# Closing products of a four-layer trunk: weight units of 256 columns over 4 row tiles, or of 512 columns over 2

## The chip, the cores and the metric

The kernel runs on one core of a Trainium2 chip, in one launch. The metric is device microseconds (us) of that core, as the median of repeated runs. The engines are named as in the profile: PE is TensorE's matmul, PEld its weight load, DVE is VectorE, ACT is ScalarE, POOL is GpSimd, SP is the queue that issues all DMAs here.

## What is computed

One inference step of a trunk of four layers over 640 tokens (128 context, 512 latent), 1024 features. Each layer has a token mixer (differential attention, neighbourhood attention, grouped-query attention, Hyena) and then a squared-ReLU MLP, each followed by a gated residual addition and a LayerNorm:

```python
for i in range(DEPTH):                     # 4 layers
    mod = jnp.split(silu(c) @ ada_w[i] + ada_b[i], 6)
    o = mixer_i(modulate(x, mod[0], mod[1]))           # ends in a product with w_o: 1024 x 1024
    x = layer_norm(DN_ALPHA * x + mod[2] * o, ln_g[i, 0], ln_b[i, 0])
    h = modulate(x, mod[3], mod[4])
    f = jnp.square(jax.nn.relu(h @ mlp_w1[i])) @ mlp_w2[i]   # 1024 x 4096, 4096 x 1024
    x = layer_norm(DN_ALPHA * x + mod[5] * f, ln_g[i, 1], ln_b[i, 1])
```

All products with weights are made from high and low parts in float32r, three passes each (`mm3`, L473 to L477): high times high, high times low, low times high.

## The kernel before

**Weight stream.** Every weight matrix is cut on the host into units of 128 x 1024 floats (512 KB). One list, `wlist`, written by `weight_order`, gives the order in which they are used. `wget` takes the next unit and, while at it, has the next `ahead=2` units converted (`w_convert`: ACT copies the high part, L451, DVE or POOL subtracts for the low part, L453) and the ones behind them loaded (`w_issue`, L422, from SP into 3 raw buffers). A converted unit, 128 x 2 x 1024, stands in one of 5 buffers with the tag `hl`. Other things stand there as well: in the MLP of layer 0 the hidden activations of the Hyena filter network (`hab`), which all taps read, and the filter weights being worked on; in the MLPs of layers 1 and 2 the DFT tables.

**Units.** A unit for a feature-major product (`unit_a`: `w1`, `qk`, `hy_in`) has 8 row tiles by 128 columns. A unit for a token-major product (`unit_b`) has 4 row tiles by 256 columns: values, the closing product of the MLP (`w2`), the output projections (`wo`).

**MLP.** The 4096 hidden features go in 8 chunks of 512. For a chunk the four units of `w1` are multiplied (320 tokens per matmul) and their result is squared on ACT and split into `ff`. Then the four units of `w2` of the chunk before are used: for each unit (a quarter q of the 1024 output features) and each of five token tiles t, `w2_group` makes 12 matmuls of 256 columns (4 row tiles, three passes) into one PSUM bank, and `residual` takes it out: DVE multiplies with the gate (L655), then one addition in four on DVE and the others on POOL add to the residual stream (L662). `any1` rotates over four PSUM banks. Between units `side` does the work that the list has there: the adaLN modulation of the next layer (`ada_step`, four DVE instructions of 512 columns for each, L543, ended after 8 by PE, L548), and for the Hyena layer filter weights, taps (`tap_step`, every third group; two matmuls of 512 columns, L1581 and L1582) and DFTs (`hy_dft`).

**Output projections.** They are made in two halves of the features. The first half is a generator (`out_steps`) that gives PE work between attention units: one step, one group (t, q), counted as 1280. The second half and the last chunk of the MLP are made in `sublayer_end`, token tile by token tile, each followed by LayerNorm (`ln_norm`), transposes (L724) and modulation (`ln_out`). For the last token tile `quick` puts all additions on DVE.

**Buffers for short tiles.** 16 buffers of 128 x 640 floats (tag `S`, `self.S`) hold gates, LayerNorm gains, adaLN weights and temporaries. `gtmp`, the product with the gate, has 3 buffers of 256 columns of its own. The framework fixes each engine's order of instructions when the program is built, and an instruction that waits holds up what stands behind it on its engine.

Of the kernel before, what the change touches and what calls it, by code (L numbers as in the profile page):

```python
# [10 lines left out]
F32 = mybir.dt.float32  # L11
# [7 lines left out]
P = 128  # L19
# [10 lines left out]
DEPTH = 4  # L30
# [14 lines left out]
OL0 = 20  # L45
OL1 = 6
# [25 lines left out]
# ---------------------------------------------------------------- host layout and shape constants  # L72
# [127 lines left out]

def prepare(inp):
# [15 lines left out]
    d["w2"] = np.stack([np.stack([unit_b(g["mlp_w2"][l], 4 * ch, q * 256) for ch in range(8) for q in range(4)]) for l in range(DEPTH)])  # L217
# [8 lines left out]
    for nm, wo in (("da", g["da_w_o"][0]), ("na", g["na_w_o"][0]), ("gq", g["gq_w_o"][0][rows]), ("hy", g["hy_w_o"][0])):  # L226
        d[nm + "_o"] = np.stack([unit_b(wo, 4 * kh, q * 256) for kh in range(2) for q in range(4)])
# [51 lines left out]
# ---------------------------------------------------------------- device program  # L279
class Trunk:  # L280
    HL = HLN
    RAW = RAWN
    NS = 16
# [27 lines left out]
    # ---- small helpers  # L311
# [33 lines left out]
    # ---- weight stream  # L345
    def weight_order(self):
        out = []
        for n, l in enumerate(self.layers):
# [46 lines left out]
    def head_order(l):  # L395
        """order of the projections: values of a group of four heads, queries and keys of a pair"""
# [59 lines left out]
    def reach(self, i, n):  # L456
        """end of the first n weights of the stream from i on that need a buffer of it"""
# [14 lines left out]
    # ---- products in three passes  # L472
# [6 lines left out]
    def span_a(self, ps, t, c0, c1):  # L479
        """feature-major product of one unit with tokens c0 to c1; yields now and then"""  # L480
# [6 lines left out]
    # ---- adaLN  # L487
# [30 lines left out]
    def ada_load(self, l, step):  # L518
        """weights of one step: 128 rows (or the bias row) of two neighbouring modulations"""
# [10 lines left out]
    def ada_step(self, raw, l, m, k):  # L530
        """128 rows of a modulation weight times their factors, added up row by row; the sum over partitions ends it"""
# [39 lines left out]
    def ada_gen(self, l, ahead, p0, p1):  # L571
        """pairs p0 to p1 of modulations of a layer; one step per yield, its weights loaded `ahead` steps before"""
# [44 lines left out]
    def load_ln(self, l, j, last=False):  # L617
        """gain and bias of a LayerNorm on all partitions, scaled for the residual stream"""
# [1611 lines left out]
```

## Time and profile before

| | |
|---|---|
| time, median of 3 runs | 3496.15 us (3494.53 to 3499.4) |
| span of the profiled execution | 3487.9 us, 8.25 us under that median |
| busy: PE, PEld, DVE | 3324.3, 3183.9, 2600.0 us |
| busy: ACT, POOL | 1512.3, 1003.6 us |
| matmuls | 25288, as many weight loads |
| mean granted clock of TensorE | 0.986 of full speed |

The span runs from the first to the last instruction of the profiled execution; its own total was not recorded, so what lies around the span is taken as the difference to the median. A matmul's duration in the profile (280 ns for 256 columns) includes its way through the array and overlaps with its neighbours: the rate is read from start to start.

### The profile page before, as it was taken

Reading aid. Unit: us, or ns where it says so; the run is one execution under the profiler, and the core shown is the slowest. Engines: PE = TensorE matmul, PEld = TensorE weight load, DVE = VectorE, ACT = ScalarE, POOL = GpSimd, SP = SyncE. Lnnn points to the kernel's source line nnn. Section 1 sums busy time; section 2 is a strip of 40 time slices with the busy share of each in tenths; the row PEclk is TensorE's granted clock in tenths of the full one; section 3 lists DMA queues with packets and bytes.
Section 4 is the critical chain, followed back from the end, with each engine's and each line's share of the span. In section 5 each row is a group of like instructions: output and inputs, shape, how many; then the busy total and the mean of one; then the engine's idle time right before and its main releaser. Section 6 shows DMA issues by size and latency. Waiting matters only on the chain. (4 is left out here: it accounts for less than half of the span.)

```text
span 3487.9 us, 63715 instructions
## 1 busy us (share of the span) xinstructions
PE 3324.3 (95%) x25288; PEld 3183.9 (91%) x25288; DVE 2600.0 (75%) x4691; ACT 1512.3 (43%) x2700; POOL 1003.6 (29%) x961
## 2 busy tenths in 40 slices
PE   8998999999999989999998999999998999999998
PEld 6878889998999889999988889999998998999998
DVE  4777888788676678777688878777859888945457
ACT  3555453333356654433335665333324333432322
POOL 0333334334354453122252014232334112500002
PEclk9999999999999999999999999999999999999999
DMA  7343134545242324555412112545523224222221
GB/s 271 122 133 108 49 129 165 171 166 175 82 130 77 104 75 158 187 169 197 143 60 69 31 53 94 184 152 182 164 93 123 81 81 152 88 91 79 85 75 54
DMA packets 157644, 418.97 MB, mean 120 GB/s; under 512 B 19550, under 2 KB 29414, under 8 KB 154270
## 3 DMA queue, kind: packets, MB, share of 16 engines
q1 hardware_dynamic: 157344, 414.88, 35.8%
q8 instruction: 199, 3.26, 0.4%
q14 instruction: 101, 0.83, 0.1%
HBM read 371.20 MB, written 34.05 MB: 116 GB/s over the span
## 5 line engine op out<-in xcount | busy, mean ns | idle before, releaser
L662 POOL TENSOR_TENSOR r<-r,gtmp 128x256 f32<-128x256 f32 x444 | 437.8, 999 | 1127.6 <-DVE gtmp L655 1097.3
L453 DVE TENSOR_TENSOR hl<-raw,hl 128x1024 fp32r<-128x1024 f32 x390 | 506.6, 1301 | 322.1 <-ACT hl L451 320.6
L475 PE MATMUL w<-hl,ff 128*128 128x256 f32 x2560 | 716.0, 280 | 7.2 <-DVE gtmp L655 7.1
L476 PE MATMUL w<-hl,ff 128*128 128x256 f32 x2560 | 715.2, 279 | 2.5 <-DVE hl L453 2.4
L477 PE MATMUL w<-hl,ff 128*128 128x256 f32 x2560 | 713.9, 279 | 0.0
L451 ACT CAST hl<-raw 128x1024 fp32r<-128x1024 f32 x411 | 430.2, 1048 | 638.3 <-PE w L477 508.9
L475 PE MATMUL w<-hh,hl 128*128 128x320 f32 (+2 forms) x2048 | 637.7, 312 | 0.2
L476 PE MATMUL w<-hl,hl 128*128 128x320 f32 (+2 forms) x2048 | 634.9, 310 | 1.8 <-DVE hl L736 1.8
L477 PE MATMUL w<-hh,hl 128*128 128x320 f32 (+2 forms) x2048 | 634.3, 310 | 0.0
L475 PEld LDWEIGHTS w<-hl,ff 128*128 128x128 f32 x2560 | 481.0, 188 | 12.1 <-DVE gtmp L655 9.9
L476 PEld LDWEIGHTS w<-hl,ff 128*128 128x128 f32 x2560 | 480.9, 188 | 5.0 <-DVE hl L453 3.3
L477 PEld LDWEIGHTS w<-hl,ff 128*128 128x128 f32 x2560 | 479.9, 187 | 0.0
L543 DVE SCALAR_TENSOR_TENSOR ada<-adaw,sil,ada 128x512 f32<-128x512 f32 x504 | 388.2, 802 | 88.2 <-DMA adaw<-in_ada_w 80.5
L475 PEld LDWEIGHTS w<-hh,hl 128*128 128x128 f32 x2048 | 387.2, 189 | 13.8 <-issue 8.4
L476 PEld LDWEIGHTS w<-hl,hl 128*128 128x128 f32 x2048 | 387.2, 189 | 3.1 <-DVE hl L736 3.0
L477 PEld LDWEIGHTS w<-hh,hl 128*128 128x128 f32 x2048 | 387.0, 189 | 0.8 <-issue 0.8
L655 DVE TENSOR_TENSOR gtmp<-w,gate 128x256 f32<-128x256 f32 x640 | 261.1, 415 | 162.4 <-PE w L477 152.1
L874 ACT ACTIVATE fx<-w 128x640 f32<-128x640 f32 (+2 forms) x136 | 91.6, 673 | 454.2 <-PE w L477 435.3
L475 PE MATMUL qk<-hh,hl 128*128 128x320 f32 (+2 forms) x672 | 216.5, 322 | 6.7 <-DVE gtmp L655 3.9
L476 PE MATMUL qk<-hl,hl 128*128 128x320 f32 (+2 forms) x672 | 211.0, 314 | 0.0
L477 PE MATMUL qk<-hh,hl 128*128 128x320 f32 (+2 forms) x672 | 211.0, 314 | 0.0
L475 PE MATMUL wo<-hl,oh 128*128 128x256 f32 x640 | 184.0, 288 | 8.9 <-DVE gtmp L655 5.8
(344 smaller groups left out, 7132.4 us busy)
## 6 DMA issues: line engine op xcount, KB each, us to landing
raw<-in_w SPq DMA_DIRECT2D x256, 512.0 KB
adaw<-in_ada_w SPq DMA_DIRECT2D x288, 256.0 KB
adaw<-in_ada_w SPq DMA_DIRECT2D x16, 1024.0 KB
raw<-ab_d SPq DMA_DIRECT2D x32, 512.0 KB
raw<-in_hy_in SPq DMA_DIRECT2D x24, 512.0 KB
adaw<-in_ada_s SPq DMA_DIRECT2D x8, 1024.0 KB
raw<-in_da_qk SPq DMA_DIRECT2D x16, 512.0 KB
gate<-gate_d SPq DMA_DIRECT2D x32, 256.0 KB
```

Source lines behind the costliest of these rows:

```text
L451: self.nc.scalar.copy(t[:, 0], raw)
L453: sub(t[:, 1], raw, t[:, 0].bitcast(F32))
L475: mm(ps, w[0], x[0], start=start, stop=False)
L476: mm(ps, w[0], x[1], start=False, stop=False)
L477: mm(ps, w[1], x[0], start=False, stop=stop)
L543: nc.vector.scalar_tensor_tensor(out=y, in0=raw[h], scalar=x, in1=y, op0=ALU.mult, op1=ALU.add)
L655: nc.vector.tensor_mul(tmp, ps, self.gate[2 * s + q // 2][:, (q % 2) * 256:(q % 2) * 256 + 256])
L662: eng.tensor_add(rv, rv, tmp)
L874: nc.scalar.activation(x, src, AF.Relu)
```

## The change

Units of `w2` and of the output projections have 2 row tiles by 512 columns (`unit_w`). A product of a token tile and 512 output columns takes two units, so it is 4 row tiles by three passes again: 12 matmuls, of 512 columns, into one PSUM bank. Gate and residual addition take 512 columns. For the last token tile (`quick`) each half is still made and taken out in two pieces of 256. `gtmp` comes from the `S` buffers, of which there are 17. In the MLP, two units are fetched together and used for five token tiles; the side work comes after the third of the five and at the end, and the list has it after every second unit of `w2`. Steps of the first half of the output projection are twice as large and half as many. The rest of the diff takes comments and docstrings out.

```diff
+def unit_w(w, k0, c0):
+    return w[k0 * P:(k0 + 2) * P, c0:c0 + 512].reshape(2, P, 512).transpose(1, 0, 2).reshape(P, 1024)
...
-    d["w2"] = np.stack([np.stack([unit_b(g["mlp_w2"][l], 4 * ch, q * 256) for ch in range(8) for q in range(4)]) for l in range(DEPTH)])
+    d["w2"] = np.stack([np.stack([unit_w(g["mlp_w2"][l], 4 * ch + 2 * kp, h * 512) for ch in range(8) for h in range(2) for kp in range(2)]) for l in range(DEPTH)])
...
-        d[nm + "_o"] = np.stack([unit_b(wo, 4 * kh, q * 256) for kh in range(2) for q in range(4)])
+        d[nm + "_o"] = np.stack([unit_w(wo, 4 * kh + 2 * kp, h * 512) for kh in range(2) for h in range(2) for kp in range(2)])
...
-    NS = 16
+    NS = 17
...
-                        if 0 < ch < 8:
-                            out += ada[:1] + side[i // 4].get(4 * (ch - 1) + i % 4, [])
-                            ada = ada[1:]
+                        if 0 < ch < 8 and (i < 4 or i % 2):
+                            for n in range(4 * (ch - 1) + (i % 4 if i < 4 else i - 5), 4 * (ch - 1) + i % 4 + 1):
+                                out += ada[:1] + side[i // 4].get(n, [])
+                                ada = ada[1:]
...
+    def wide_group(self, us, x, t, h, quick=False):
+        c = slice(t * P, (t + 1) * P)
+        for c0, w in ((0, 256), (256, 256)) if quick else ((0, 512),):
+            ps = self.any1([P, w], "w2")
+            for k in range(4):
+                u, f = us[k // 2], slice(k % 2 * 512 + c0, k % 2 * 512 + c0 + w)
+                self.mm3(ps, (x[:, 0, k, c], x[:, 1, k, c]), (u[:, 0, f], u[:, 1, f]), k == 0, k == 3)
+            self.residual(ps, t, h, c0, w, quick)
...
-        tmp = self.base.tile([P, 256], F32, tag="gtmp", bufs=3, name=f"gtmp{self.tn}")
-        nc.vector.tensor_mul(tmp, ps, self.gate[2 * s + q // 2][:, (q % 2) * 256:(q % 2) * 256 + 256])
-        rv = self.r[:, t, q * 256:(q + 1) * 256]
+        tmp = self.S(F32, "gtmp", w)
+        nc.vector.tensor_mul(tmp, ps, self.gate[2 * s + h][:, c0:c0 + w])
+        rv = self.r[:, t, h * 512 + c0:h * 512 + c0 + w]
...
-            for q in range(4):
-                u = self.wget(("w2", l, 4 * (ch - 1) + q))
+            for h in range(2):
+                us = [self.wget(("w2", l, 4 * (ch - 1) + 2 * h + kp)) for kp in range(2)]
                 for t in range(NT):
-                    w2_group(u, ch - 1, q, t)
-                    groups += 1
-                    if self.taps and groups % TSTEP == 0:
+                    self.wide_group(us, ff[ch - 1], t, h)
+                    groups += 2
+                    if self.taps and groups % TSTEP < 2:
                         self.tap_step()
+                    if t == 2:
+                        self.side(2)
                 self.side()
...
-    def side(self):
-        while self.wlist[self.wi][0] in ("ada", "hyw", "hyt", "hyd", "hyc"):
+    def side(self, parts=1):
+        n = 0
+        while self.wlist[self.wi + n][0] in ("ada", "hyw", "hyt", "hyd", "hyc"):
+            n += 1
+        for _ in range(-(-n // parts)):
```

In `out_steps` the loop over four quarters becomes a loop over two halves with two units each, and a step counts as 2560; `OL0`, `OL1` and the bounds on `out_left` are halved.

## Rows read from the trace of the kernel before

**Rows 1.** The page, part 1: busy us, share of the span, instructions.
```profile
PE 3324.3 (95%) x25288; PEld 3183.9 (91%) x25288; DVE 2600.0 (75%) x4691; ACT 1512.3 (43%) x2700; POOL 1003.6 (29%) x961
```

**Rows 2.** Windows of three closing stretches: busy us by engine, clock, DMA.
```profile
700.50:733.00 32.50, 31.21 (x254) 30.25 (x252) 30.23 (x53) 11.96 (x17) 17.72 (x17) 1.00 0.48 161
733.00:739.00 6.00, 3.70 (x12) 1.04 (x13) 6.00 (x11) 1.55 (x2) 4.16 (x4) 1.00 0.42 146
1424.00:1456.00 32.00, 30.70 (x257) 30.37 (x256) 30.77 (x48) 8.75 (x10) 15.06 (x13) 1.00 0.49 156
```

**Rows 3.** Groups of PE instructions: busy us, mean ns, idle before and its enders.
```profile
L475 PE MATMUL w<-hl,ff 128*128 128x256 f32 x2560 | 716.0, 280 | 7.2 <-DVE gtmp L655 7.1
L476 PE MATMUL w<-hl,ff 128*128 128x256 f32 x2560 | 715.2, 279 | 2.5 <-DVE hl L453 2.4
...
L475 PE MATMUL wo<-hl,oh 128*128 128x256 f32 x640 | 184.0, 288 | 8.9 <-DVE gtmp L655 5.8 <-ACT oh L1049 2.6 <-ACT o L1128 0.3
...
L548 PE MATMUL ada<-ada,ones 128*32 128x512 f32 x144 | 30.2, 605 | 5.7 <-DVE ada L543 5.6
```

**Rows 4.** Timeline of PE in layer 0: start us, duration us, what.
```profile
704.77 0.40 PE L1581 MATMUL filt<-hl,hab 128*128 128x512 f32 x1
...
705.25 0.28 PE L475 MATMUL w<-hl,ff 128*128 128x256 f32 x1
...
709.49 0.40 PE L1581 MATMUL filt<-hl,hab 128*128 128x512 f32 x1
...
709.95 0.28 PE L475 MATMUL w<-hl,ff 128*128 128x256 f32 x1
...
714.03 0.40 PE L1581 MATMUL filt<-hl,hab 128*128 128x512 f32 x1
...
714.49 0.28 PE L475 MATMUL w<-hl,ff 128*128 128x256 f32 x1
```

**Rows 5.** Timeline of PE in layer 3, where a run of one shape begins.
```profile
3078.26 0.28 PE L475 MATMUL w<-hl,ff 128*128 128x256 f32 x1
...
3106.53 0.31 PE L475 MATMUL w<-hh,hl 128*128 128x320 f32 x1
...
3134.69 0.28 PE L475 MATMUL w<-hl,ff 128*128 128x256 f32 x1
```

**Rows 6.** Groups of DVE instructions by form.
```profile
L543 DVE SCALAR_TENSOR_TENSOR ada<-adaw,sil,ada 128x512 f32<-128x512 f32 x504 | 388.2, 802 | 88.2 <-DMA adaw<-in_ada_w 80.5 <-ACT ln_b L787 6.4 <-ACT ada L541 1.0
L655 DVE TENSOR_TENSOR gtmp<-w,gate 128x256 f32<-128x256 f32 x640 | 261.1, 415 | 162.4 <-PE w L477 152.1 <-POOL r L662 9.9
L662 DVE TENSOR_TENSOR r<-r,gtmp 128x256 f32<-128x256 f32 x336 | 168.5, 503 | 7.7
...
L742 DVE TENSOR_TENSOR r<-r,ln_g 128x512 f32<-128x512 f32 x35 | 29.7, 869 | 0.0
...
L1585 DVE TENSOR_TENSOR win<-win,filt 128x512 f32<-128x512 f32 x40 | 26.9, 673 | 0.3 <-PE filt L1582 0.3
```

**Rows 7.** Groups of POOL instructions by form.
```profile
L662 POOL TENSOR_TENSOR r<-r,gtmp 128x256 f32<-128x256 f32 x444 | 437.8, 999 | 1127.6 <-DVE gtmp L655 1097.3 <-DVE m L2015 24.8 <-DVE rs L693 4.8
...
L753 POOL TENSOR_TENSOR r<-r,ln_g 128x512 f32<-128x512 f32 x8 | 11.1, 1384 | 419.9 <-ACT r L698 419.9
```

**Rows 8.** Waits: us in total, times, longest us.
```profile
ACT hl L451 <- PE w L477: 508.9, 98, 8.4
```

**Rows 9.** Timelines of ACT and of DVE in layer 1: one conversion.
```profile
1432.22 1.05 ACT L451 CAST hl<-raw 128x1024 fp32r<-128x1024 f32 x1 [4.02 <-PE w L477]
...
1434.68 1.75 DVE L453 TENSOR_TENSOR hl<-raw,hl 128x1024 fp32r<-128x1024 f32 x1
```

**Rows 10.** The chain that ended last, end of layer 2's mixer: start us, us.
```profile
2111.88 0.45 PE lnt L724 x4
...
2116.09 1.92 POOL r L662 x2
```

More of the change, by code (lines that the diff above doesn't have):

```diff
@@ L44 @@
 AHD = 1
-OL0 = 20
-OL1 = 6
+OL0 = 10
+OL1 = 3
 WS = (0, 1, 2)
@@ L802, in sublayer_end @@
         self.after = self.spill if spill else self.ln_residual
-    def out_group(self, units, oh, t, qs, quick=False):
-        c = slice(t * P, (t + 1) * P)
-        for q in qs:
-            u = units[q]
-            ps = self.any1([P, 256], "wo")
-            for k in range(4):
-                f = slice(k * 256, (k + 1) * 256)
-                self.mm3(ps, (oh[:, 0, k, c], oh[:, 1, k, c]), (u[:, 0, f], u[:, 1, f]), k == 0, k == 3)
-            self.residual(ps, t, q, quick)
     def out_half(self):
@@ L820, in out_first @@
     def out_first(self, l, nm, split):
-        self.out_left = 4 * NT
+        self.out_left = 2 * NT
         return self.out_steps(l, nm, split)
@@ L833, in out_steps @@
         yield 1
-        for q in range(4):
-            u = {q: self.wget((nm + "_o", q), ahead=1)}
-            if q == 1:
-                self.load_gates(l, 0, (1,))
-                gate.update(self.gate)
-                self.gate = gate
-            for t in range(NT):
-                if q == 0 and t + 2 < NT:
+        for h in range(2):
+            us = [self.wget((nm + "_o", 2 * h + kp), ahead=1) for kp in range(2)]
+            for t in range(NT):
+                if h == 0 and t == 2:
+                    self.load_gates(l, 0, (1,))
+                    gate.update(self.gate)
+                    self.gate = gate
+                if h == 0 and t + 2 < NT:
                     split(oh, 0, t + 2)
-                self.out_group(u, oh, t, (q,))
+                self.wide_group(us, oh, t, h)
                 self.out_left -= 1
-                yield 1280
+                yield 2560
         self.scale_r = False
@@ L850, in out_rest @@
         self.load_ln(l, 0)
-        while self.out_left > 6:
+        while self.out_left > 3:
             next(first)
@@ L860, in out_rest @@
         units = [self.wget((nm + "_o", 4 + q), ahead=1) for q in range(4)]
-        self.sublayer_end(l, 0, lambda t, i: self.out_group(units, oh, t, (2 * i, 2 * i + 1), t == NT - 1))
+        self.sublayer_end(l, 0, lambda t, i: self.wide_group(units[2 * i:2 * i + 2], oh, t, i, t == NT - 1))
     def mlp(self, l, nxt, last):
@@ L907, in w1_first @@
             self.settle()
-        def w2_group(u, ch, q, t, quick=False):
-            ps = self.any1([P, 256], "w2")
-            c = slice(t * P, (t + 1) * P)
-            for kk in range(4):
-                f = slice(kk * 256, (kk + 1) * 256)
-                self.mm3(ps, (ff[ch][:, 0, kk, c], ff[ch][:, 1, kk, c]), (u[:, 0, f], u[:, 1, f]), kk == 0, kk == 3)
-            self.residual(ps, t, q, quick)
         for ch in range(8):
@@ L938, in mlp @@
         units = [self.wget(("w2", l, 28 + q), ahead=1) for q in range(4)]
-        def close(t, i):
-            for q in (2 * i, 2 * i + 1):
-                w2_group(units[q], 7, q, t, t == NT - 1)
-        self.sublayer_end(l, 1, close, last, nxt in (1, 3))
+        self.sublayer_end(l, 1, lambda t, i: self.wide_group(units[2 * i:2 * i + 2], ff[7], t, i, t == NT - 1), last, nxt in (1, 3))
     def v_gen(self, nm, gr, vv, chunks, state):
@@ L1990, in close @@
         self.debt += CRATE
-        while self.debt > 0 and self.k.out_left > 6:
+        while self.debt > 0 and self.k.out_left > 3:
             self.debt -= next(self.first)
```

5 lines of the change are left out of this document (2 added, 3 removed).

## The prediction, made before the changed kernel ran

> **What bounds the kernel now.** I read the page first: PE is busy for 95% of the span and PEld for 91%, DVE for 75% [rows 1]. A busy PE need not be a PE at its rate, so I then took the timeline of PE and looked at starts. In layer 3, 240 matmuls of 256 columns take 28.27 us, 117.8 ns each, and the 192 of 320 columns behind them 28.16 us, 146.7 ns each [rows 5]: back to back, nothing in between. There PE's streaming is the bound. The windows show the second limit: in the closing stretches of layers 0 and 1, DVE is busy for 30.2 of 32.5 us and 30.8 of 32 us, almost as long as PE, and just behind the first of these PE was busy for only 3.7 of 6 us while DVE was busy for all 6 [rows 2]. The groups of PE say what that is worth: the idle time that ends with DVE's gate product or with its adaLN sum is 7.1, 5.8 and 5.6 us [rows 3], 18.5 us in the whole kernel. So little is to be had behind PE; what counts is the rate of PE and what newly holds it up.
>
> **Term 1: matmuls, -7 us.** There are 640 + 160 groups of 12 matmuls [rows 3]. The quick tiles keep 4 groups in each of 8 sublayer ends, 384 matmuls; the other 9216 of 256 columns become 4608 of 512. As many columns are streamed. Only a cost per matmul can be saved, and the rows give it twice. Directly: in layer 0 three pairs of 512-column matmuls of the filter work stand in the stream, 480, 460 and 460 ns a pair [rows 4], 240, 230 and 230 ns each, mean 233.3. The 36 matmuls of 256 columns between them took 117.8 and 113.3 ns each [rows 4]. By a line: from 256 to 320 columns the interval grows by 28.9 ns, 0.452 ns a column, which leaves 2.2 ns fixed and gives 233.4 ns at 512. Two matmuls of 256 cost 235.6 ns, or about 234.8 with layer 0's faster stretches counted in. I take 1.5 ns saved per wide matmul: 4608 x 1.5 = 7 us. Bounds from the same rows: 230 ns would give 4608 x 5.6 = 26 us faster, 240 ns 4608 x 4.4 = 20 us slower.
>
> 4608 weight loads go too. I cost them at nothing: a load runs under the matmul before it, and four transposes of 128 columns start 113 ns apart [rows 10], which is below 117.8. If that cover is thinner than it looks, the gain is the first rival's.
>
> **Term 2: DVE and POOL, -9 us.** 768 gate products of 415 ns [rows 6] become 384 of 512 columns. Their nearest row is a 512-column product out of PSUM, 673 ns [rows 6]: 319 us become 258, 60 saved. The additions on DVE, 503 ns at 256 and some 869 at 512 [rows 6], save perhaps 20 us more. POOL's, 999 ns at 256 and 1384 ns in a 512-column row [rows 7], go from 438 us to some 310. Nearly all of it lies under PE. In one chunk of layer 0 (some 33 us), 20 x 415 ns become 10 x 673, 1.6 us less on an engine that is 93% busy. I give half of the 18.5 us that PE waits for DVE today: 9. Bounds: 0 and 18.5.
>
> **Term 3: sublayer ends, -3 us.** Here the chain runs through DVE and POOL; at the end of layer 2's mixer two POOL additions take 1.92 us of it [rows 10]. One of 512 columns is 1.4 to 1.5 us by rows 7. Seven ends with POOL on the path, 0.4 us each: 3 us. The last token tile is still taken in 256s, so the last wait before the LayerNorm is the same, and so is the kernel's tail. Bounds: 0 and 7.
>
> **Term 4: the weight buffers, +8 us.** This is the cost. A group now needs two units at once, and both are held for five tiles, 14.1 us, where one was held for 7.1. With 5 `hl` buffers, of which layer 0 keeps 2 (activations, filter weights) and layer 1 up to 2 (DFT tables), the pair leaves one to convert ahead. Already ACT's conversions wait 98 times, 508.9 us, for PE to release a buffer [rows 8]; today that is free, since the unit is needed 7 us later. A conversion seen whole took from 1432.22 to 1436.43 us, 4.2 us, because DVE had other work in front [rows 9]. Now the first buffer of a pair is released when PE is half through its last group, 1.4 us before the next half begins. Where nothing was converted ahead the wait is up to 4.2 - 1.4 = 2.8 us. What queues behind it: PE's next products, and on ACT the squares and on DVE the gate products behind the conversion. There are 28 halves in layers 0 and 1, so the bounds are 0 and 78 us. I expect most to have one unit ready; and with four PSUM banks PE can make the first unit's products of the next tiles meanwhile. I take 8 waits of 1 us.
>
> **Term 5: +1 us.** `gtmp` now competes for the `S` buffers that adaLN weights are loaded into; there is one buffer more and about one more in use. DVE already waits 80.5 us for those loads [rows 6]. If they came a tenth later, 8 us would be the price on DVE, under PE in most places. I take 1. **At nothing:** the larger steps between attention units, the adaLN steps that come two to a half (same count), the loads (same bytes through SP, in the same order of use). What hides them is PE's own work: the idle time before `wo` products is 8.9 us in all [rows 3]; coarser steps could double or halve it, 9 us either way.
>
> Sum: -7 - 9 - 3 + 8 + 1 = -10 us. On the span, 3487.9 - 10 = 3478; with the 8.25 us to the median, 3486.
>
> **Rivals.**
>
> *The loads set the pace (3452 us).* If the 117.8 ns are mostly a load (113 ns apart in the transposes, [rows 10]) and not streaming, the wide matmul gains more. The granted clock is at its upper level, 2.4 GHz, in these stretches [rows 2]: 0.417 ns a column; 320 columns then have 13.3 ns of fixed cost, 512 columns take 226.7, and 4608 x 8.9 = 41 us are saved in place of 7: -44 us. For it: PEld's 91%. Against it: no 512-column row is below 230 ns. The Trainium skill (Perfetto Trace Analysis, Identifying the Most-Contended Engine) counts LDWEIGHTS busy time, not matmul busy time, as the measure of how near TensorE is to its limit, and so speaks for this rival; the 512-column rows of this trace speak against it.
>
> *No buffer ahead (3522 us, the other side).* In layers 0 and 1, the pair leaves no converted unit at 20 of the 28 halves, and PE stands for 2.2 us at each: +44 in place of +8, a sum of +26 us. It turns the sign where the waits come to more than 18 us, 0.64 us a half. For it: the 98 waits, and conversions that take 4.2 us. Against it: in layers 2 and 3 there is room, and the order of PE can be bent around a late unit. The Trainium skill (Perfetto Trace Analysis, Optimization Strategy) reads a gap that repeats on the busiest engine as a sign of too few buffers; no such gap stands in the trace of before, it would be new.
>
> *Slow wide stream (3513 us).* All wide matmuls run like the slowest pair, 240 ns: +20 in place of -7, a sum of +17. For it: that pair stands in the 117.8 ns regime, which layer 3 has throughout. Against it: two pairs of three.
>
> *Nothing to measure (3489 to 3503 us).* Streaming the same, DVE's relief off the path or eaten by term 4.
>
> **How the numbers follow.** The forecast, small and faster, has 0.33, with a range of its own of 3468 to 3489; loads 0.10; nothing 0.25; no buffer 0.20; slow stream 0.12. 0.2% is 7 us, about what a measurement of this kernel can tell from no change. Faster: 0.33 + 0.10 = 0.43; same 0.25; slower 0.20 + 0.12 = 0.32. The range, 3458 to 3524, takes in the forecast, no change, and both slower rivals; it leaves out the loads' case and the upper end of term 4, together under 0.2.
>
> **What would show it.** Term 1: starts of `w` matmuls of 512 columns in layer 3 at 233 ns (227 or 240 for the rivals). Term 2: 416 gate products, the 512s near 675 ns, and less idle PE before L548. Term 3: shorter gaps before L724. Term 4: PE idle that ends with DVE's conversion (L453), 2.4 us now in that group of products [rows 3], should rise to some 8; at 40 the buffer rival is right, and the waits would stand in layers 0 and 1 and not in layer 3. The prediction is wrong if the wide interval is off by 3 ns (14 us), or if another order of the engines moves the attention stages by more than the 9 us that I allow.

## The result, and the profile after

The changed kernel takes 3585.87 us (median of 4 runs, 3580.0 to 3589.75) against 3496.8 us (4 runs, 3494.53 to 3499.4): a ratio of 1.026, 95% interval 1.0248 to 1.0272. It is 89 us slower, outside the predicted range of 3458 to 3524. The profiled execution has a span of 3584.6 us, 96.7 more than the one before.

The page, part 1, of the changed kernel:

```profile
PE 3363.5 (94%) x20680; PEld 2987.4 (83%) x20680; DVE 2563.1 (72%) x4145; ACT 1511.0 (42%) x2700; POOL 924.5 (26%) x739
```

Beside [rows 1]: 4608 matmuls and as many loads fewer, as forecast; DVE 37 us and POOL 79 us less busy, where the forecast was some 80 and 128. Yet PE is busy for 39 us *more*, and idle for 57 us more. To see where, take one window from the first `w1` matmul to the last `w2` matmul of each layer. First the kernel before, layers 0 to 3 (window, length, busy us of PE, PEld, DVE, ACT, POOL, clock, DMA):

```profile
440.44:955.09 514.65, 497.33 (x3634) 475.78 (x3633) 406.85 (x652) 206.10 (x298) 188.95 (x176) 0.99 0.45 149
1291.09:1796.24 505.15, 497.26 (x3794) 488.49 (x3793) 383.43 (x569) 198.76 (x275) 147.88 (x135) 0.99 0.47 157
2126.40:2626.79 500.39, 490.35 (x3747) 480.85 (x3745) 376.49 (x564) 190.57 (x262) 153.86 (x135) 1.00 0.45 149
3011.49:3473.24 461.75, 456.41 (x3475) 455.14 (x3472) 266.10 (x460) 140.91 (x189) 36.62 (x24) 0.99 0.23 76
```

The same windows of the changed kernel, and three short ones inside layer 0:

```profile
447.60:1011.86 564.26, 515.56 (x2698) 439.80 (x2697) 405.17 (x555) 207.23 (x297) 172.91 (x118) 0.95 0.41 136
1349.75:1875.78 526.03, 506.17 (x2858) 446.13 (x2857) 382.97 (x472) 198.89 (x275) 124.75 (x77) 0.99 0.46 151
2204.99:2721.35 516.36, 501.65 (x2811) 442.63 (x2809) 380.02 (x467) 190.79 (x262) 123.48 (x77) 0.98 0.43 144
3113.57:3570.87 457.30, 451.72 (x2538) 412.13 (x2537) 243.97 (x307) 141.71 (x191) 40.82 (x26) 0.99 0.24 76
...
489.60:517.60 28.00, 28.00 (x190) 27.78 (x190) 15.70 (x21) 11.43 (x17) 0.00 (x0) 1.00 0.57 194
587.60:643.60 56.00, 51.15 (x233) 39.55 (x232) 42.87 (x59) 18.60 (x25) 20.67 (x15) 0.94 0.47 156
545.60:559.60 14.00, 5.98 (x13) 1.29 (x12) 9.59 (x15) 1.06 (x2) 4.79 (x4) 0.63 0.37 131
```

The MLPs of layers 0, 1 and 2 are 49.6, 20.9 and 16.0 us longer; layer 3's, the only one with no side work (adaLN of a next layer, filter taps, DFTs), is 4.5 us shorter. What lies between the windows, the mixers, grew by 7.2, 1.9, -0.9 and 7.5 us. So the loss is in the MLPs with side work, not in wide products as such.

PE's stream itself did well. From the timeline of PE, where a half of wide products begins and where the next `w1` unit begins, in layer 3 (start us, duration us):

```profile
3182.31 0.40 PE L480 MATMUL w<-hl,ff 128*128 128x512 f32 x1
...
3209.80 0.31 PE L480 MATMUL w<-hh,hl 128*128 128x320 f32 x1
```

120 matmuls in 27.49 us are 229.1 ns each, against 235.6 ns for two of 256 columns [rows 5]: 6.5 ns saved. Layer 3 is the best case. In the MLPs of layers 0 to 2, where nothing held them up, matmuls of 256 columns started 116.6 to 117.4 ns apart and those of 512 229.1 to 229.9, so 3 to 6 ns are saved there, and some 23 us in the whole kernel; 6.5 ns everywhere would be 30. What PE waited for, in groups that answer to [rows 3] (busy us, mean ns, idle before and its enders):

```profile
L481 PE MATMUL w<-hl,ff 128*128 128x512 f32 (+1 forms) x1312 | 510.9, 390 | 7.6 <-DVE hl L458 7.4
L480 PE MATMUL w<-hl,ff 128*128 128x512 f32 (+1 forms) x1312 | 509.7, 389 | 16.7 <-DVE gtmp L669 16.7
...
L553 PE MATMUL ada<-ada,ones 128*32 128x512 f32 x144 | 55.7, 671 | 23.1 <-DVE ada L548 21.2 <-DVE gtmp L669 1.7
```

Waits of PE in the kernel before (us in total, times, longest):

```profile
PE lnt L724 <- ACT r L698: 23.6, 11, 4.5
...
PE w L476 <- DVE hl L736: 1.8, 5, 0.8
```

And PE's waits in the changed kernel:

```profile
PE w L480 <- DVE gtmp L669: 17.1, 13, 4.3
PE w L481 <- DVE hl L750: 13.1, 4, 3.3
...
PE w L480 <- DVE win L1581: 9.7, 4, 4.0
PE lnt L738 <- ACT r L712: 9.2, 4, 2.3
```

At the sublayer ends the wait before the transposes became shorter (23.6 to 9.2 us), but that of the `w1` products behind them for the modulated input became longer (1.8 to 13.1). The adaLN sums (5.6 to 21.2 us) and the gate products (7.1 to 16.7 us, 17.1 with those before `w1` products) got worse. One such stall, in layer 0, on three engines of the changed kernel. The timeline of PE (start us, us, what, idle before and who ended it):

```profile
766.74 0.39 PE L1578 MATMUL filt<-hl,hab 128*128 128x512 f32 x1
771.38 0.80 PE L480 MATMUL w<-hl,ff 128*128 128x512 f32 x1 [4.25 <-DVE gtmp L669]
771.98 0.63 PE L481 MATMUL w<-hl,ff 128*128 128x512 f32 x1
772.40 0.63 PE L482 MATMUL w<-hl,ff 128*128 128x512 f32 x1
```

The timeline of DVE at that place:

```profile
765.05 0.67 DVE L1581 TENSOR_TENSOR win<-win,filt 128x512 f32<-128x512 f32 x1
768.45 0.75 DVE L548 SCALAR_TENSOR_TENSOR ada<-adaw,sil,ada 128x512 f32<-128x512 f32 x1 [2.72 <-DMA adaw<-in_ada_w]
...
770.66 1.27 DVE L669 TENSOR_TENSOR gtmp<-w,gate 128x512 f32<-128x512 f32 x2
```

The timeline of SP's queue ahead of it:

```profile
758.70 0.33 SPq L427 DMA_DIRECT2D raw<-in_w  x1
...
763.34 0.33 SPq L1592 DMA_DIRECT2D abc_d<-ab  x1
763.76 0.38 SPq L427 DMA_DIRECT2D raw<-in_w  x1
764.20 1.40 SPq L437 DMA_DIRECT2D adaw<-in_ada_w  x3
```

And what SP waited for from 758 to 772 us (us in total, times, longest):

```profile
SPq L1592 <- DVE ab L1586: 12.7, 3, 5.1
SPq L427 <- DVE hl L458: 2.9, 1, 2.9
```

Read backwards: PE stands for 4.25 us before a wide product, until the first of two gate products has emptied its bank. DVE has these gate products *behind* adaLN steps: it waits 2.72 us for the weights of one of their instructions, and then does that one, another and parts of a filter tap before the first gate product. SP issued three of those loads only from 764.20 on, behind a store of filter taps and a raw weight load. The store had waited 3.2 us for DVE before 763.34 (the rest of the 12.7 us falls behind the loads), and the raw load before it, at 758.70, 2.9 us for a conversion by DVE: the ring is closed.

It is not that loads came later on the whole. DVE's wait for adaLN weights in the changed kernel (us in total, times, longest), against 80.5 us before [rows 6]:

```profile
DVE ada L548 <- DMA adaw<-in_ada_w: 73.3, 31, 7.4
```

What grew is PE's wait behind DVE.

The clock adds to it. From 762.0 to 766.7 us the granted clock was 1.00; from 771.3 to 775.0, behind the stall, it was 0.56, and PE's matmuls start 0.42 us apart (771.98 to 772.40), not 0.23. Around 546 us, where PE was busy for 6.0 of 14 us, it was 0.63; over layer 0's MLP it was 0.95, before 0.99. With two levels, 2.4 and 1.2 GHz, the clock records of the two traces give 51 us of this stage at the lower one, in place of 10. PE is busy there for 18.2 us more and idle for 31.4 us more. So about a third of this stage's 49.6 us, or a little more, is slower matmuls, and the rest is standing (an estimate from these windows).

### The profile page after: what moved, and what is told of

Read it like the earlier page. It is cut to its first block, busy times and chain, and to the rows that moved or that the text cites. A ratio compares the mean times of both kernels' runs of the same rounds, so it can differ in the third digit from the quotient of the medians.

```text
span 3584.6 us, 53289 instructions
## 1 busy us (share of the span) xinstructions
PE 3363.5 (94%) x20680; PEld 2987.4 (83%) x20680; DVE 2563.1 (72%) x4145; ACT 1511.0 (42%) x2700; POOL 924.5 (26%) x739
## 4 chain that ended last, share of the span: by engine, by line
PE 54%; DVE 16%; issue 4%; POOL 3%; ACT 2%; DMA 2%; SPq 0%; DVEq 0%; POOLq 0%; ACTq 0%
PE w L481 12%; PE w L480 12%; PE w L482 12%; DVE ada L548 2%; DVE gtmp L669 2%; DVE hl L458 2%; PE s L2006 2%; PE pv L2053 2%; PE ptp L1057 2%; POOL r L676 2%; PE qk L480 1%; PE qk L481 1%; PE qk L482 1%; DVE r L676 1%; DVE hl L750 1%
## 5 line engine op out<-in xcount | busy, mean ns | idle before, releaser
L676 POOL TENSOR_TENSOR r<-r,gtmp 128x512 f32<-128x512 f32 x222 | 353.3, 1596 | 1286.4 <-DVE gtmp L669 1249.5
L480 PE MATMUL w<-hh,hl 128*128 128x320 f32 (+2 forms) x2048 | 645.1, 315 | 11.0 <-DVE win L1581 9.7
L481 PE MATMUL w<-hl,hl 128*128 128x320 f32 (+2 forms) x2048 | 642.6, 314 | 13.1 <-DVE hl L750 13.1
L482 PE MATMUL w<-hh,hl 128*128 128x320 f32 (+2 forms) x2048 | 641.6, 313 | 1.9 <-DVE hl L458 1.9
L480 PE MATMUL w<-hl,ff 128*128 128x512 f32 (+1 forms) x1312 | 509.7, 389 | 16.7 <-DVE gtmp L669 16.7
L481 PE MATMUL w<-hl,ff 128*128 128x512 f32 (+1 forms) x1312 | 510.9, 390 | 7.6 <-DVE hl L458 7.4
L482 PE MATMUL w<-hl,ff 128*128 128x512 f32 (+1 forms) x1312 | 509.5, 389 | 0.0
L548 DVE SCALAR_TENSOR_TENSOR ada<-adaw,sil,ada 128x512 f32<-128x512 f32 x504 | 414.2, 864 | 80.6 <-DMA adaw<-in_ada_w 73.3
L480 PEld LDWEIGHTS w<-hh,hl 128*128 128x128 f32 x2048 | 392.5, 192 | 29.3 <-DVE win L1581 13.2
L482 PEld LDWEIGHTS w<-hh,hl 128*128 128x128 f32 x2048 | 391.9, 191 | 7.5 <-issue 5.0
L669 DVE TENSOR_TENSOR gtmp<-w,gate 128x512 f32<-128x512 f32 (+1 forms) x416 | 272.8, 661 | 103.0 <-PE w L482 102.7
L480 PEld LDWEIGHTS w<-hl,ff 128*128 128x128 f32 x1312 | 247.5, 189 | 77.8 <-DVE gtmp L669 20.8
L481 PEld LDWEIGHTS w<-hl,ff 128*128 128x128 f32 x1312 | 247.8, 189 | 65.1 <-DVE hl L458 13.6
L482 PEld LDWEIGHTS w<-hl,ff 128*128 128x128 f32 x1312 | 247.7, 189 | 53.5 <-issue 4.2
L480 PEld LDWEIGHTS qk<-hh,hl 128*128 128x128 f32 x672 | 129.3, 192 | 23.9 <-issue 19.6
```

Source lines behind the costliest of these rows:

```text
L480: mm(ps, w[0], x[0], start=start, stop=False)
L481: mm(ps, w[0], x[1], start=False, stop=False)
L482: mm(ps, w[1], x[0], start=False, stop=stop)
L548: nc.vector.scalar_tensor_tensor(out=y, in0=raw[h], scalar=x, in1=y, op0=ALU.mult, op1=ALU.add)
L669: nc.vector.tensor_mul(tmp, ps, self.gate[2 * s + h][:, c0:c0 + w])
L676: eng.tensor_add(rv, rv, tmp)
```

## The experiments

In the source of the experiments `W2` and `WO` name the layers whose closing MLP product and output projection are wide, `GT` is the number of buffers that `gtmp` has of its own (0: it comes from `S`), `NS` and `HLN` are the numbers of `S` and of weight buffers. The changed kernel is `W2 = WO = (0, 1, 2, 3)`, `GT = 0`, `NS = 17`, `HLN = 5`; with `W2 = WO = ()`, `GT = 3`, `NS = 16` it is the kernel before. Each diff is against the kernel named. The third column is the difference to runs of the kernel before on the same chip; changes from one kernel to another are taken from this column, where the changed kernel stands at +89.1.

| run | median us | against before | ratio, 95% interval |
|---|---|---|---|
| e1 only `w2` wide | 3576.61 | +81.1 | 1.0236 (1.0222 to 1.0250) |
| e2 only `wo` wide | 3523.70 | +28.2 | 1.0082 (1.0068 to 1.0096) |
| e3 only `w2` of layer 3 wide | 3497.91 | +2.4 | 1.0012 (1.0003 to 1.0021) |
| e4 changed, 256-column matmuls | 3594.21 | +98.7 | 1.0288 (1.0273 to 1.0304) |
| e5 before, `gtmp` in `S` | 3505.66 | +9.6 | 1.0029 (1.0019 to 1.0038) |
| e6 changed, gate in 256s, own buffers | 3577.16 | +81.1 | 1.0229 (1.0212 to 1.0246) |
| e7 before, 4 weight buffers | 3585.60 | +89.5 | 1.0255 (1.0240 to 1.0270) |
| e8 changed, adaLN loads first | 3564.55 | +68.5 | 1.0197 (1.0182 to 1.0212) |
| e9 changed, 14 `S` | 3588.78 | +94.1 | 1.0275 (1.0259 to 1.0290) |
| e10 changed, 14 `S`, 6 weight buffers | 3598.87 | +104.2 | 1.0305 (1.0291 to 1.0318) |
| e11 before, adaLN loads first | 3498.29 | +3.6 | 1.0012 (1.0004 to 1.0021) |
| e12 as e3, gate as before | 3490.86 | -3.8 | 0.9991 (0.9982 to 0.9999) |
| e13 changed, thin adaLN | 3494.09 | -1.0 | 1.0000 (0.9991 to 1.0010) |
| e14 before, thin adaLN | 3463.79 | -31.3 | 0.9908 (0.9893 to 0.9923) |
| e15 before, pair list | 3562.32 | +67.2 | 1.0186 (1.0171 to 1.0202) |
| e16 e6 and e8 together | 3563.20 | +68.1 | 1.0194 (1.0177 to 1.0211) |
| e17 changed, adaLN beside `w1` | 3508.82 | +14.8 | 1.0043 (1.0029 to 1.0058) |
| e18 as e12, adaLN beside `w1` | 3469.12 | -24.9 | 0.9929 (0.9916 to 0.9941) |

### Which part of the change (e1 to e4)

```diff
 e1, against the changed kernel
-WO = (0, 1, 2, 3)
+WO = ()
 e2, against the changed kernel
-W2 = (0, 1, 2, 3)
+W2 = ()
```

> The changed kernel with the output projections as before (units of 256 columns, steps of 1280); the closing MLP product stays wide. By stage, the changed kernel lost 82 us in the MLPs and 14 us in the mixers and ends. If all the loss of the MLPs comes from the wide MLP product itself (theories A, buffers, and B, side work, alike), this kernel stands near 3572 us, 14 less than the changed one. If the wide projections also spoil the MLPs that follow, by a shifted order of the engines, it stands below 3555.

> The kernel before with only the output projections wide. Both theories leave the MLPs alone here: 3496 + 14 = 3510 us if the mixers' loss stays, 3490 if the loss of the mixers was only a late start that the MLPs handed on (1152 wide matmuls at some 6.5 ns saved each are 7 us).

The wide MLP product alone costs 81 us, the wide projections alone 28; they don't add up to 89, so the parts share a cost. e2 came out above both of its forecasts: its MLPs, narrow as before, did not stay as they were, layer 0's was 14 us longer and layer 1's 10. (The 1152 wide matmuls in its forecast should be 864.)

```diff
 e3, against the changed kernel
-W2 = (0, 1, 2, 3)
-WO = (0, 1, 2, 3)
+W2 = (3,)
+WO = ()
```

> The kernel before with only the closing MLP product of layer 3 wide. That MLP has no side work, and no buffer is kept for activations or tables. A (a pair of units leaves too few weight buffers, everywhere) would show some of the loss here too: 3496 to 3510 us. B (the loss is that of side work standing beside the pairs) gives the streaming gain alone, 864 wide matmuls x 6.5 ns = 5.6 us: 3491 us. In the changed kernel this stage was 4.4 us shorter.

Layer 0's and layer 3's MLP in this kernel:

```profile
443.57:970.75 527.18, 498.68 (x3634) 482.43 (x3633) 401.58 (x652) 206.70 (x298) 193.71 (x176) 0.97 0.43 146
...
3027.43:3483.01 455.58, 450.22 (x2539) 410.68 (x2536) 242.73 (x308) 141.29 (x190) 37.88 (x24) 0.99 0.23 77
```

By its time alone e3 would speak for theory A. The windows say otherwise: layer 3 gains 6.2 us, all that the stream should bring (its MLP has 936 wide matmuls, not 864: 936 x 6.5 = 6.1). But layer 0, narrow in every instruction, loses 12.5: something other than width and pairs came with the change.

```diff
 e4, against the changed kernel, in wide_group
-            for k in range(4):
-                u, f = us[k // 2], slice(k % 2 * 512 + c0, k % 2 * 512 + c0 + w)
-                self.mm3(ps, ...
+            for d in range(0, w, 256):
+                for k in range(4):
+                    u, f = us[k // 2], slice(k % 2 * 512 + c0 + d, k % 2 * 512 + c0 + d + 256)
+                    self.mm3(ps[:, d:d + 256], ...
```

> The changed kernel in everything (pairs of units, 512-column bank, 512-column gate product and addition, side work in the same places, S buffers), but each wide matmul is made as two of 256 columns. If the loss comes with the staging (A and B), the 30 us that the wide stream saved go as well: 3586 + 30 = 3616 us. If the wide matmuls are themselves what costs (fewer, longer instructions, more of the clock's lower level), this kernel comes back towards before: under 3520 us.

Only 10 us slower than the changed kernel, between the two forecasts. So wide matmuls are not the trouble, and of what they save, 23 to 30 us, the larger part had been lost already. Layer 3's MLP gives back 5 us here; layer 0's is even 8 us shorter than in the changed kernel.

### Theory A: too few weight buffers (e7, e9, e10)

```diff
 e7, against the kernel before
-HLN = 5
+HLN = 4
 e9, against the changed kernel
-NS = 17
+NS = 14
 e10, against e9
-HLN = 5
+HLN = 6
```

> The kernel before with 4 weight buffers in place of 5 and nothing else. Holding two units of the closing product in place of one takes one buffer away during that product. A: taking one away for good costs the narrow kernel as much or more: 3550 us or above, with layer 0's MLP (which keeps activations in one) hit first. If the number of buffers is not what hurts: 3496 to 3510 us.

> The changed kernel with 14 S buffers in place of 17 and nothing else: the control for the next kernel, which needs the room. C (short tiles are scarce, and scarcer with the gate product among them): slower than the changed kernel, 3590 to 3620 us. If S buffers are not scarce: 3580 to 3590.

> The changed kernel with 6 weight buffers and 14 S buffers: against the control it has one weight buffer more and no other difference. A (the pair holds one buffer too many; one buffer is worth 90 us to the narrow kernel): 40 to 80 us less than the control. B (late side work alone): within 15 us of the control.

e7 looked like a proof: one buffer fewer costs the narrow kernel 89.5 us. But its loss stands elsewhere: 21 us in layer 0's MLP, 30 in layer 1's, none in layer 2's, and 10, 17, 5 and 12 in the mixers. e9 is 5 us slower than the changed kernel, so three `S` buffers are worth little there. And e10 takes the proof back: one weight buffer *more* does not help the wide kernel, it is 10 us slower than its control. The wait in question (us in total, times, longest), in e9:

```profile
ACT hl L462 <- PE w L488: 482.3, 119, 14.1
```

And in e10:

```profile
ACT hl L462 <- PE w L488: 442.0, 107, 14.7
```

The conversions wait 40 us less for PE, and nothing comes of it; the kernel before has 508.9 us of this wait [rows 8] and is the faster one. Theory A falls as the cause of this loss; whether a sixth buffer helps once the adaLN steps are moved (e17) was not run. The Trainium skill (Perfetto Trace Analysis, Optimization Strategy) says that a gap repeating on the busiest engine can mean too few buffers; here a gap stands in six chunks of layer 0 (PE busy for 6.0 to 11.7 of 14 us in the worst window of each), and the buffer nearest at hand was not the cause.

### Theory C: the short tiles (e5, e6, e12)

```diff
 e5, against the kernel before
-NS, GT = 16, 3
+NS, GT = 17, 0
 e6, against the changed kernel (its wide_group); e12, against e3
-NS, GT = 17, 0
+NS, GT = 16, 3
...
-            self.residual(ps, t, h, c0, w, quick)
+            for d in range(0, w, 256):
+                self.residual(ps[:, d:d + 256], t, h, c0 + d, 256, quick)
```

> The kernel before with one edit: the 256-column product with the gate comes from the S buffers, of which there are 17, in place of 3 buffers of its own. Where only layer 3's MLP was made wide, and where only the projections were, the MLP of layer 0 was 12.5 and 14.2 us longer although it was narrow; what it shared with the changed kernel was this. C (the shared short-tile buffers cost by themselves): 3496 plus 12 to 22 us, 3508 to 3518, with layer 0's MLP some 12 us longer. If those 12 us were an accident of a shifted order of the engines: 3496 us, within 5.

Layer 0's MLP in e5:

```profile
443.14:971.29 528.15, 499.60 (x3634) 483.75 (x3633) 401.08 (x652) 206.77 (x297) 194.48 (x176) 0.97 0.43 146
```

It is 13.5 us longer than before, and the kernel 9.6 us (lower than expected, since layer 2's MLP came out 5.5 us shorter). The cost that term 5 of the prediction names is real.

> The changed kernel with wide matmuls and pairs of units, but the product with the gate and the addition in two pieces of 256 columns, in 3 buffers of their own, with 16 S buffers as before. C: the sharing's cost goes, 12 to 22 us less than the changed kernel, 3564 to 3574 us. A (pairs leave too few weight buffers) and B (side work) keep the rest of the 90 us. If the wide eviction relieved DVE by what term 2 said, 9 us come back on top: 3573 to 3583. If the sharing and the wide eviction together were the whole loss, under 3510.

8 us better than the changed kernel, a little short of the mark, and the mixers come back. The windows of layers 0, 2 and 3 in e6:

```profile
443.93:996.84 552.91, 507.09 (x2698) 435.61 (x2697) 409.83 (x653) 208.18 (x298) 190.18 (x177) 0.97 0.41 139
...
2195.30:2714.55 519.25, 499.81 (x2810) 440.89 (x2809) 387.81 (x565) 190.54 (x262) 135.66 (x136) 0.98 0.42 144
3099.39:3558.00 458.61, 450.93 (x2538) 411.26 (x2537) 250.68 (x457) 140.90 (x190) 38.23 (x24) 0.99 0.22 76
```

Layer 0's mixer ends 3.5 us after the time of before, not 7.2, and layer 3's takes 384.84 us, as before (384.70), not 392.22. e6 changes two things at once, the buffers and the width of the pieces; e5, with the buffers alone, made these two mixers 2.7 and 5.8 us longer, so most of it is the buffers. The MLPs stay slow.

> The kernel before with the closing MLP product of layer 3 alone in wide matmuls and pairs; the gate product and the addition stay in pieces of 256 columns with their own 3 buffers, and 16 S buffers stay. The wide MLP of layer 3 was 6.2 us shorter, and the shared S buffers cost 10 us by themselves. A and C together: 3496 - 6 = 3490 us, faster than both kernels. If the shared buffers were not what cost in the layer 3 experiment: 3497.

3.8 us faster than the kernel before, with an interval that just leaves out 1; the forecast of 3490 held.

### Theory B: side work that comes late (e8, e11, e16, e15)

```diff
 e8, against the changed kernel; e11, against the kernel before; e16, against e6 (in wget)
+        self.ada_issue(self.reach(self.wi, AAH) )
         self.w_convert(self.reach(i + 1, ahead))
         self.w_issue(self.reach(self.w_cv, raws))
-        self.ada_issue(self.reach(self.wi, AAH) )
```

> The changed kernel with one edit: the loads of the adaLN weights are issued ahead of the conversions and raw loads of the same step, so that they don't stand behind raw loads that wait for a buffer on SP's queue. B (PE waits in its fixed order for side work that comes late): the 21 us that PE waits for adaLN sums fall to some 6, and with what queues behind them the time to 3560 to 3572 us. A: no change, 3580 to 3590 us.

> The kernel before with the loads of the adaLN weights issued ahead of the conversions and raw loads of the same step. In the changed kernel this edit took 21 us off. If late adaLN loads are a thing that pairs bring (raw loads wait longer for a buffer and hold up SP's queue), the narrow kernel gains at most the 5.6 us that PE waits for adaLN sums: 3490 to 3497 us. If the order on SP was simply bad in both: 3475 to 3485.

21 us come back in the changed kernel, and PE's waits for adaLN sums fall to 13.9 us:

```profile
PE ada L559 <- DVE ada L554: 13.9, 9, 4.5
```

DVE's own wait for these loads did not fall with it:

```profile
DVE ada L554 <- DMA adaw<-in_ada_w: 83.8, 35, 8.7
```

The same edit does nothing good to the narrow kernel (+3.6 us), in which DVE waits 80.5 us for such loads without it [rows 6]. So late loads are common to both forms, and their sum does not follow the time; in the changed staging PE hangs on them.

> The changed kernel with both edits that helped: gate product and addition in pieces of 256 columns with buffers of their own (9 us less by itself), and adaLN loads issued first (21 us less by itself). If they are separate costs: 3556 us. If they are the same cost seen twice (the S buffers hold up the adaLN loads): 3564 us or more. If the remaining loss hung on both together: under 3530.

With e6's edit on top nothing more is gained (+68.1 in place of +68.5): the two are not separate costs. 68 us remain.

```diff
 e15, against the kernel before
 in weight_order: the list as in the changed kernel (side work behind every second unit of w2)
 in mlp:
             for q in range(4):
-                u = self.wget(("w2", l, 4 * (ch - 1) + q))
+                if q % 2 == 0:
+                    us = [self.wget(("w2", l, 4 * (ch - 1) + q + kp)) for kp in range(2)]
                 for t in range(NT):
-                    self.narrow_group(u, ff[ch - 1], t, q)
+                    self.narrow_group(us[q % 2], ff[ch - 1], t, q)
...
-                self.side()
+                self.side(2 - q % 2)
```

> The kernel before (units of 256 columns, one used after the other, its own gate buffers) with only the fetching of the changed kernel in the MLPs: two units are fetched together, the list has the side work behind every second unit, and it is done after the fifth and the tenth group. A second unit is converted earlier, but the first is free again after five groups as before. If list order and fetching in pairs are the main cost: 3530 to 3560 us. If holding both units for the whole half is what costs, or the width: 3496 to 3510.

The four MLPs of e15:

```profile
447.23:991.06 543.83, 507.96 (x3635) 478.51 (x3633) 406.33 (x652) 207.33 (x298) 186.79 (x176) 0.98 0.43 141
1326.81:1852.53 525.72, 510.07 (x3795) 491.75 (x3793) 384.09 (x569) 198.59 (x276) 142.83 (x135) 0.98 0.46 151
2182.88:2699.99 517.11, 501.18 (x3746) 484.08 (x3745) 380.89 (x564) 190.50 (x263) 146.94 (x135) 0.99 0.43 145
3085.06:3545.84 460.78, 455.32 (x3474) 453.95 (x3473) 266.07 (x459) 140.87 (x189) 36.66 (x24) 0.99 0.24 76
```

Same matmuls, same gate products, same buffers, the same side work in other places: and 67 us lost. Layers 1 and 2 lose 20.6 and 16.7 us, as in the changed kernel (20.9 and 16.0); layer 0 loses 29 of its 50; layer 3, with no side work, nothing. PE's waits for gate products and adaLN sums in e15:

```profile
PE w L486 <- DVE gtmp L688: 22.4, 24, 2.9
PE ada L559 <- DVE ada L554: 16.0, 12, 3.8
```

Together 38.4 us, as in the changed kernel (17.1 and 21.2), where the kernel before has 7.1 and 5.6 [rows 3]. The list and the fetching in pairs are the main cost, and only where there is side work. The two were not run apart from each other.

### The link: adaLN steps on DVE (e13, e14, e17, e18)

```diff
 e13, against the changed kernel; e14, against the kernel before
 in ada_issue:
-            if key[0] == "ada":
+            if key[0] == "ada" and key[3] in (0, KD - 1):
 in ada_step:
-        for h in range(2):
+        for h in range(2) if k in (0, KD - 1) else ():
```

> The changed kernel with six of the eight accumulation steps of each adaLN modulation of layers 1 to 3 left out, with their loads (the first and the last step and the closing sums stay, so the modulations are not those of the reference). B' (DVE, in its fixed order, stands at adaLN steps whose loads come late, and the gate products behind them hold up PE): most of the loss goes, within 30 us of the same omission in the kernel before. If adaLN is not the link, the distance stays at 70 to 90 us.

> The kernel before with the same six of eight adaLN steps and their loads left out (the modulations of layers 1 to 3 are not those of the reference): the other side of the comparison. PE waits 5.6 us for adaLN sums today, and DVE stands before gate products for 12.9 us: 3475 to 3492 us.

With thin adaLN work the distance between the two forms falls from 89 to 30 us: the omission saves the narrow kernel 31 us, more than forecast, and the wide one 90. So some 59 us of the distance hang on adaLN work, and 30 do not.

```diff
 e17, against the changed kernel; e18, against e12 (in weight_order, w2 in pairs, n the place of a unit)
-                                out += ada[:1] + side[i // 4].get(n, [])
-                                ada = ada[1:]
+                                m = 2 - i % 2 if i < 4 else int(n % 4 == 0)
+                                out += ada[:m] + side[i // 4].get(n, [])
+                                ada = ada[m:]
 and likewise where w2 is taken unit by unit
```

> The changed kernel with the adaLN steps moved, none left out: six of them stand behind the four w1 units of a chunk (two and one in turn) and one in the w2 part, in place of four and four. In the changed kernel's layer 0, DVE is busy for 15.7 of 28 us beside w1 (489.6 to 517.6 us of its span) and for 42.9 of 56 us in the two parts that follow a chunk further on; a step is four instructions of 0.86 us, 3.4 us. B' (in the w2 part, with its list in pairs, DVE's steps come late and hold up gate products and with them PE): 3520 to 3550 us. If only the amount of adaLN work on DVE counts, not where it stands: 3575 us or more.

Nothing is left out here, and the changed kernel comes down by 74 us, more than forecast. PE's waits for adaLN sums and gate products in e17:

```profile
PE ada L561 <- DVE ada L556: 7.4, 7, 2.5
...
PE w L488 <- DVE gtmp L690: 3.0, 4, 1.0
```

The windows of the MLPs of layers 0 to 2 in e17:

```profile
447.82:970.10 522.28, 497.03 (x2698) 436.92 (x2697) 402.29 (x555) 206.52 (x297) 165.04 (x118) 0.98 0.44 147
1309.16:1815.65 506.49, 497.54 (x2859) 445.09 (x2857) 371.49 (x472) 198.79 (x275) 117.41 (x77) 0.99 0.47 157
2143.68:2644.63 500.95, 491.42 (x2811) 439.74 (x2809) 365.02 (x467) 190.33 (x262) 117.89 (x77) 0.99 0.44 149
```

21.2 and 17.1 us of waiting became 7.4 and 3.0, and the three MLPs lose 42, 20 and 15 us of length. DVE does the same 504 adaLN instructions; it does fewer of them beside the gate products, and more beside `w1`, where in the changed kernel it was busy for only 15.7 of 28 us. In one chunk of layer 1 they take 8.4 us beside `w1` (1464.89 to 1494.19 us) and 16.4 beside `w2` (1494.19 to 1527.22) in the changed kernel; in e17 13.7 (1475.19 to 1507.57) and 5.4 (1507.57 to 1537.94).

> The kernel of the wide MLP product in layer 3 alone with the gate in pieces of 256 columns (3490.9 us), with the same move of the adaLN steps to the w1 units in layers 0 to 2. Leaving out six of eight steps took 31 us off the kernel before; moving three of eight steps of a chunk to where DVE has room may give a third of that: 3480 us, faster than both kernels. If the steps beside w1 come in the way of the squares and conversions there: 3495 us or more.

21 us faster than e12, 24.9 faster than the kernel before, by a ratio of 0.9929 (0.9916 to 0.9941): the fastest of all runs that leave nothing out. The move is worth 21 us to the mostly narrow kernel and 74 to the wide one. So not all of the 74 us is loss made good: the distance from the wide form to the mostly narrow one falls from 93 us (the changed kernel and e12) to 40 (e17 and e18), by 53. That fits the 59 of the thin adaLN work. The Trainium skill (Perfetto Trace Analysis, Optimization Strategy) says that kernels whose busiest engine changes over time may gain by interleaving such stretches; what was moved here is the side work of one engine from one stretch into the other, a step in that direction, and both runs gained by these numbers.

## Why the prediction was wrong, by its steps

**What bounds the kernel** was read rightly: PE's stream first, DVE close behind it in the closing stretches [rows 2]. The second half of that reading was then not used where it mattered.

**At nothing: "the adaLN steps that come two to a half (same count), the loads (same bytes through SP, in the same order of use)".** This is the step that failed. Count and bytes are the same, as it says; the places in each engine's fixed order are not. List and fetching in pairs cost 67 us without any wide product (e15). Taking adaLN steps out of the closing part gives the changed kernel 74 us back (e17), 53 more than the same move gives the mostly narrow form (e18), and issuing their loads earlier gives 21 (e8). The loads came late before as well (80.5 us of DVE's time); in the pairs' order a step that waits 2 to 3 us for its load stands in front of the gate products, and PE stands behind them. DVE was 93% busy in such a stretch before [rows 2] and is busy for 42.9 of 56 us in the changed kernel, so it is the order that costs, more than the amount of work. Cover was named (PE's own work before `wo` products), but for another stage; what stands behind each moved step on DVE was not asked.

**Term 5, +1 us:** the right mechanism, a size too small. The shared `S` buffers cost 9.6 us (e5), and the price was put "under PE in most places", where PE waited for DVE. Most of the +7.2 and +7.5 us in the mixers of layers 0 and 3, within the 9 us allowed for attention steps, comes from this too: +2.7 and +5.8 in e5, and +3.5 and +0.1 left in e6, where the gate product has buffers of its own.

**Term 1, -7 us:** right in sign, mis-sized. The interval is 229.1 ns in layer 3, 4 ns under the forecast, where the prediction's own sign of being wrong was 3; it lies nearer to the 226.7 ns of the loads' rival than to 233.3. Taken layer by layer it is some 23 us in place of 7, within the bound of 26. Layer 3 got its part (936 x 6.5 = 6.1; measured 4.5, and 6.2 in e3 and e12). The 233.3 ns were read from pairs between matmuls of 256 columns; in the changed kernel, between matmuls of 512, 17 of 32 such pairs take 226 to 228 ns, so the shape of the neighbours seems to count. Whether the gain comes from fewer loads or from fewer starts was not told apart. (The 113 ns between transposes are the 0.45 us of four in the chain; their starts in the timeline are 108.7 ns apart.) Where PE waits for DVE, the gain is not seen: e4 gives it up and loses only 10 us.

**Term 2, -9 us:** the gate product's cost was right (682 ns, forecast 673), the additions' were off by about a sixth (DVE's 711, forecast 869; POOL's 1596, forecast 1384), and the effect had the wrong sign. PE's waits for gate products and adaLN sums did not halve, they rose from 12.7 to 37.9 us in the two MLP groups of [rows 3]. Fewer and shorter instructions on DVE did not mean earlier ones; its adaLN instructions even grew, from 802 to 864 ns.

**Term 3, -3 us:** the sign that it named came, the gain did not. The wait for the LayerNorm before the transposes fell from 23.6 to 9.2 us, but the waits just behind rose: `w1` products for the modulated input from 1.8 to 13.1, the Hyena in-projection for the same from 3.7 to 7.3. In sum next to nothing is left.

**Term 4, +8 us:** PE's idle time before the group that waits for conversions rose from 2.5 to 7.6 us, about what its sign said (some 8) and 5 of the 8 us of the term; such waits stand in layers 0 to 2 and none in layer 3. e10 shows that a further buffer brings nothing. The rival "no buffer ahead" gave the right sign and was the nearest in time (3522 us, still 64 short), but that is luck: its mechanism is not the cause. Its text says that no repeating gap stands in the trace of before; a smaller one does: PE is busy for 9.4 to 11.2 of 13 us at the end of four chunks of layer 0, one of them in [rows 2].

**Left open.** e17 is still 14.8 us slower than the kernel before and 40 slower than e18, though its stream saves 23 to 30 us. Against e18, with e5's 10 us taken off and the stream that e18 lacks added, some 45 to 55 us are unexplained (an estimate). Layer 0's MLP is 20 us longer than that of e18 (e5's 13.5 may be among them); filter taps stand beside the pairs there, and they were not moved: PE's wait for their products on DVE is 9.7 us in the changed kernel and 11.8 in e17. In e15 the conversions are asked for earlier as well as the adaLN loads being issued otherwise; e8 measures only a part of that, and the rest was not told apart; nor was e15 run with its adaLN steps moved. The waits of PE named here point at the place, not at the amount: in e5 they are 33.7 us for gate products, and the kernel loses 9.6. Of e2's 28 us, e5 explains 10. The narrow kernel with moved adaLN steps and nothing wide was not run, so the share of layer 3 in e18's gain is known from e12 alone.

## What to carry to other kernels

When an edit changes only the order or the grouping of side work, cost it by where it lands on the fixed order of the engine with the least slack: list what stands behind each moved instruction, and what that instruction waits for, before writing "same count, same bytes". What a resource costs when one is taken away (89.5 us for a weight buffer) need not tell what one more would give (here nothing, in the changed kernel). And before a busy engine is relieved by making its instructions fewer, see whether other work on it can be moved to a stretch where it has room: here that was worth 21 us with narrow products in three of four layers, and 74 with wide ones in all.

## What was not expected of the hardware

Matmuls of 512 columns in float32r, in a long run of one shape, start 229.1 ns apart, less than the 230 to 240 ns seen for pairs between matmuls of 256 columns. A stall can cost twice: behind PE's 4.25 us at 771 us the granted clock fell to its lower level, and matmuls started 0.42 us apart in place of 0.23; the changed kernel's mean clock was 0.972, before 0.986. An addition on POOL grew from 999 ns at 256 columns to 1596 at 512, more than the row of another 512-column operation (1384) had led to expect.
